# Sliding-window attention in rounded fp32: stacked query halves for the scores, split products for the values

## The chip, the cores and the metric

The kernel runs on one core of a Trainium2 chip. A core has a matrix engine (TensorE; "PE" in the profile, with its weight loads as "PEld"), two engines for element-wise work that read and write both memories (VectorE "DVE", ScalarE "ACT"), GpSimd ("POOL") and a queue that issues transfers (SyncE "SP"). They run side by side and meet at semaphores; each works through its own list of instructions in order. The metric is the device time of one execution in microseconds, as the median of several runs.

## The reference

A decoder trunk of two layers on one sequence of 256 tokens with 2048 features, all in fp32. Layer 0 is a recurrent block (RG-LRU) with a SwiGLU feed-forward part of 5632 features. Then one set of keys and values is projected. Layer 1 is grouped-query attention on a sliding window, with sinks, and again a feed-forward part. The change is in the keys and values and in the attention of layer 1:

```python
k = rms_norm(k.reshape(bsz, s, N_KV_HEADS, HEAD_DIM), k_g)      # 4 key heads of 64
v = v.reshape(bsz, s, N_KV_HEADS, HEAD_DIM)
...
q = rms_norm((h @ w_q).reshape(bsz, s, N_KV_HEADS, GROUP, HEAD_DIM), q_g)   # 32 query heads
scores = einsum("bnqhgd,bnkhd->bnhgqk", q, k_band) / sqrt(HEAD_DIM)
scores = where(window_mask(nblk), scores, -1e30)
probs = softmax(concatenate([scores, sink], axis=-1))[..., :-1]
out = einsum("bnhgqk,bnkhd->bnqhgd", probs, v_band)
return x + out.reshape(...) @ w_o
```

The band of a query block of 128 tokens is its own block and the one ahead of it. So the first block has 128 keys and the second 256.

## The kernel before

Activations lie with features in the 128 rows and the 256 tokens in the columns (T = 256). Weights come in tiles of 128 rows by 1024 columns, one tile per job; `stream` (L244) runs through the jobs, loads four tiles ahead and splits three ahead.

Each operand of a large product is split into a high part that rounded fp32 (fp32r) holds exactly and a low part with the rest. A product is then the sum of high times high, high times low and low times high. `split` (L236) does this for weights, with one ScalarE copy (L241) and one VectorE subtraction (L242) per tile; `split_act` (L321) does it for activations, high part in columns 0 to 255 and low part in columns 256 to 511 of a slot. The projections' products stand in `products` (L261, the products themselves on L269). A job of a projection is 24 products of 256 columns.

Everything else is a background task, written as a generator. `run_bg` (L192) is called twice in a job. It steps tasks as long as an estimated credit of VectorE and ScalarE time lasts; the helpers `a`, `tt`, `ts` and others add to the estimates, and `pe(ns)` takes off what TensorE spends on background products. From the key projection on, the credits are 740 and 900 ns per half job (`LATER`, L59). One way leads around the credit: `need(v)` (L205) is called by a job for its input and steps all tasks, whatever the credit, until that input is ready. Behind the generators the tile framework orders each engine's instructions and sets the waits.

The stage of the change has three parts. `kv` (L642), 8 jobs, projects keys and values. The keys of each key head are normalised, multiplied out of `sl` by a selecting matrix (L693) so that both 64-row halves of PSUM hold the same head, and split. Before, `kd[h]` is a pair of slots (high and low) in which rows 0 to 63 hold the keys in columns 0 to 255 and rows 64 to 127 hold them in columns 256 to 511, with zeros elsewhere; so one product gives the scores of two query heads. Values stay in fp32, 256 columns per token block.

`attn` (L758) has 32 jobs of w_q in four groups of eight, then w_o in four groups of eight. When a group of w_q ends, its `task` squares and splits the four tiles of q (two heads each), sums the squares on TensorE (L895, the group's statistics), makes the scales and spawns four `head_pair`s (L768), sixteen in all. A pair makes the scores of both token blocks (L784 to L786), scales them, adds the mask and takes the maximum (L798), takes the exponentials, scales by the reciprocal sums, transposes the probabilities (L832), copies them to a slot, multiplies by the values (L851 to L853, two heads into the two halves of the PSUM rows) and splits the result as `at[k]`. A job c of w_o's first group needs `at[2c]` and `at[2c+1]`; the last group of w_q ends just ahead of it.

PSUM has eight banks: four for the running group of a projection, up to four for the tasks.

## Time and profile before

| what | value |
|---|---|
| median of 3 runs | 1999.63 us (1999.16 to 2003.5) |
| profiled execution | 1999.26 us, span 1997.5 us |
| TensorE busy | 1987.8 us, 16795 instructions |
| VectorE busy | 1282.1 us |
| ScalarE busy | 1077.6 us |
| keys and values (first to last product) | 1018 to 1041.5 us |
| w_q and the head pairs | 1041.5 to 1206 us |
| granted TensorE clock | full throughout |

In the views below, a row of the timeline gives start, length, engine, line, operation, result and operands, shapes and count. Lengths of TensorE, VectorE and ScalarE instructions overlap those of their neighbours; what an instruction costs in a stream is the distance from its start to the next one's. In a line by form, the two numbers behind the bar are the busy time of the group and the mean length of one in ns. A plain fp32 product shows as two records, a rounded one as one.

### The profile page before, as it was taken

To read this page: it belongs to the slowest core of one execution; us is meant where nothing else is said; L and a number is where in the kernel's file an instruction comes from. 1 tells how busy PE (TensorE), PEld (TensorE's weight loads), DVE (VectorE), ACT (ScalarE), POOL (GpSimd) and SP (SyncE) were. 2 spreads that over 40 slices of the span, in tenths; PEclk is the share of its full clock that TensorE was granted. 3 is DMA by queue.
4 is the path that set the end of the run, shared out by engine and by line. 5 is a ranking of instruction groups with operands and counts; after the bars stand their busy time and mean duration, and the time that the engine had idled before them with its cause. 6 is when DMAs were issued, how large, how long until landed. Compare 5 with 4: busy or idle time off the path is not lost.

```text
span 1997.5 us, 40277 instructions
## 1 busy us (share of the span) xinstructions
PE 1987.8 (100%) x16795; PEld 1955.1 (98%) x16795; DVE 1282.1 (64%) x2062; ACT 1077.6 (54%) x1624; POOL 0.2 (0%) x4
## 2 busy tenths in 40 slices
PE   8999999999999999999999999999999999999999
PEld 8999999999999999999999999999999999999999
DVE  8989867556556656545768786765565566554543
ACT  7798655445444444434556775554454454444342
POOL 0000000000000000000000000000000000000000
PEclk9999999999999999999999999999999999999999
DMA  7655655655656566566564335655655665666663
GB/s 268 199 183 177 202 195 188 196 191 190 200 191 197 193 192 198 191 193 197 192 189 141 122 116 169 191 194 191 195 191 195 195 195 191 195 195 202 206 204 128
DMA packets 105015, 376.58 MB, mean 189 GB/s; under 512 B 11648, under 2 KB 13824, under 8 KB 104832
## 3 DMA queue, kind: packets, MB, share of 16 engines
q1 hardware_dynamic: 104832, 374.01, 58.1%
q8 instruction: 131, 2.15, 0.4%
q14 instruction: 52, 0.43, 0.1%
HBM read 371.86 MB, written 2.10 MB: 187 GB/s over the span
## 4 chain that ended last, share of the span: by engine, by line
PE 99%; ACT 0%; DMA 0%; DVE 0%; issue 0%
PE b L269 94%; PE b L545 1%; PE b L832 1%; PE b L740 1%; PE b L895 0%; PE b L851 0%; PE b L784 0%; PE b L786 0%; PE b L785 0%; PE b L853 0%; PE b L852 0%; PE b L749 0%; PE b L750 0%; PE b L751 0%; DMA x<-in_x 0%; ACT hi L241 0%
## 5 line engine op out<-in xcount | busy, mean ns | idle before, releaser
L269 PE MATMUL b<-s,hi 128*128 128x256 f32 (+1 forms) x10423 | 1430.2, 284 | 6.6 <-ACT hi L241 5.7
L269 PEld LDWEIGHTS b<-s,hi 128*128 128x128 f32 x10423 | 1322.5, 188 | 33.9 <-ACT hi L241 6.0
L242 DVE TENSOR_TENSOR lo<-raw,hi 128x1024 fp32r<-128x1024 f32 (+1 forms) x705 | 861.0, 1222 | 661.6 <-ACT hi L241 658.1
L241 ACT ACTIVATE hi<-raw 128x1024 fp32r<-128x1024 f32 (+1 forms) x705 | 746.1, 1059 | 774.7 <-PE b L269 744.3
L269 PE MATMUL b<-s,lo 128*128 128x256 f32 x5504 | 824.4, 277 | 0.0
L269 PEld LDWEIGHTS b<-s,lo 128*128 128x128 f32 x5504 | 716.4, 188 | 0.0
L105 ACT ACTIVATE t<-b 128x256 f32<-128x256 f32 x130 | 48.8, 384 | 62.2 <-PE b L269 37.9
L105 ACT ACTIVATE h<-h 128x256 f32<-128x256 f32 (+1 forms) x104 | 38.9, 375 | 21.1 <-DVE h L114 21.1
L105 ACT ACTIVATE s<-h 128x256 fp32r<-128x256 f32 (+1 forms) x106 | 42.7, 413 | 13.4 <-DVE h L114 10.9
L105 ACT ACTIVATE s<-s 128x256 f32<-128x256 f32 (+1 forms) x112 | 41.2, 415 | 4.0 <-DVE s L118 3.3
L114 DVE TENSOR_TENSOR h<-b,rstd 128x256 f32<-128x256 f32 x102 | 41.6, 415 | 0.0
L105 ACT ACT_TABLE_LOAD x31 | 39.8, 1283 | 1.3 <-PEq L1000 0.7
L114 DVE TENSOR_TENSOR h<-h,rstd 128x256 f32<-128x256 f32 x92 | 38.3, 420 | 1.5
L118 DVE SCALAR_TENSOR_TENSOR s<-x,par,s 128x256 fp32r<-128x256 f32 x80 | 36.7, 479 | 3.9 <-ACT s L105 3.9
L105 ACT ACTIVATE s<-x,par 128x256 fp32r<-128x256 f32 x80 | 37.9, 497 | 2.3 <-DVE x L114 1.8
L114 DVE TENSOR_TENSOR h<-b,t 128x256 f32<-128x256 f32 x90 | 37.5, 417 | 0.0
L114 DVE TENSOR_TENSOR s<-s,s 128x256 fp32r<-128x256 f32 (+1 forms) x80 | 31.0, 419 | 8.8 <-ACT s L105 8.6
L114 DVE TENSOR_TENSOR s<-h,s 128x256 fp32r<-128x256 f32 x88 | 36.6, 417 | 0.0
L114 DVE TENSOR_TENSOR h<-h,h 128x256 f32<-128x256 f32 x88 | 36.4, 415 | 0.1
L105 ACT ACTIVATE s<-b 128x384 f32<-128x384 f32 (+3 forms) x70 | 28.4, 428 | 10.3 <-PE b L853 5.6
L105 ACT ACTIVATE s<-s,h 128x128 f32<-128x128 f32 x64 | 28.3, 444 | 6.2 <-DVE h L123 6.2
L114 DVE TENSOR_TENSOR x<-x,b 128x256 f32<-128x256 f32 x64 | 25.2, 415 | 8.9 <-PE b L269 8.9
(99 smaller groups left out, 610.4 us busy)
## 6 DMA issues: line engine op xcount, KB each, us to landing
raw<-in_ffn_in SPq DMA_DIRECT2D x352, 512.0 KB, 3.5
raw<-in_ffn_out SPq DMA_DIRECT2D x176, 512.0 KB, 4.2
raw<-in_lru_in SPq DMA_DIRECT2D x63, 512.0 KB, 3.8
raw<-in_lru_out SPq DMA_DIRECT2D x32, 512.0 KB, 3.4
raw<-in_w_q SPq DMA_DIRECT2D x32, 512.0 KB, 3.3
raw<-in_w_o SPq DMA_DIRECT2D x32, 512.0 KB, 3.5
raw<-in_gate SPq DMA_DIRECT2D x8, 512.0 KB, 4.0
raw<-in_kv SPq DMA_DIRECT2D x8, 512.0 KB, 4.3
```

Source lines behind the costliest of these rows:

```text
L105: self.nc.scalar.activation(out, in_, func, **kw)
L114: self.nc.vector.tensor_tensor(out, a, b, op)
L118: self.nc.vector.scalar_tensor_tensor(out, a, s, b, op0, op1)
L241: self.nc.scalar.activation(hi[:, q], raw[:, q], AF.Copy)
L242: self.nc.vector.tensor_tensor(lo[:, q], raw[:, q], hi[:, q].bitcast(F32), ALU.subtract)
L269: self.nc.tensor.matmul(ps[f][:, 0:c1 - c0], w, x2[k][:, c0:c1], start=f not in begun, stop=last and all(q[1] != f for q in todo[n + 1:]))
L545: nc.tensor.matmul(ps[j][:, 0:T], (hi if high else lo)[:, c:c + P], x2[kt][:, q:q + T], start=kt == 0 and high > q, stop=kt == 1 and not high)
L740: nc.tensor.matmul(ps[f][:, 0:T], w0, x2[kt][:, q:q + T], start=k0 + kt == 0 and high > q, stop=k0 + kt == ND - 1 and not high)
L832: nc.tensor.transpose(p[:, j * P:(j + 1) * P], sc[hh][:, j * P:(j + 1) * P], one)
```

## The change

Keys. `kd[h]` becomes one slot: both 64-row halves hold the same keys, high parts in columns 0 to 255 and low parts in columns 256 to 511. The eight slots with zeros, and the clearing, are gone.

Queries. Each head of a tile of q gets its own 256 columns. Its high part lies in the 64 rows that it came in, its low part in the other 64. With such a block as weights, one product with the high keys gives high times high plus low times high in one sum over the rows, and one with the low keys adds the rest (low times low included). Per pair these are four products of 128 columns for the first token block and four of 256 for the second, in place of three of 256 and three of 512.

Values. They are scaled as before and then split, per key head 64 columns of high parts beside 64 of low parts. The transposed probabilities are split as well. The four transposes of each head's first two parts go to one bank, the two of the third to another. Their product with the values is: both value parts times the high probabilities (L852, 512 columns; L855, 256), and the high values times the low probabilities (L853, L854, weights of 64 columns). The result has its high-value part in PSUM rows 0 to 63 and its low-value part in rows 64 to 127. Two ScalarE copies and two VectorE adds of 64 rows join them for the two heads, and then the split follows.

```diff
             def task():
...
-                    self.ts(self.v[b].ap, self.v[b].ap, self.rstd[r][:, T + b:T + b + 1], None, ALU.mult)
+                    raw = vs[:, b * T:(b + 1) * T]
+                    self.ts(raw, raw, self.rstd[r][:, T + b:T + b + 1], None, ALU.mult)
+                    raw = raw.rearrange("p (h n) -> p h n", n=HD)
+                    q = self.v[b].ap.rearrange("p (h c n) -> p h c n", c=2, n=HD)
+                    self.a(q[:, :, 0], raw)
+                    self.tt(q[:, :, 1], raw, q[:, :, 0].bitcast(F32), ALU.subtract)
...
-                    kh, kl = self.kd[h].ap
-                    for i in range(2):
-                        q, c = slice(64 * i, 64 * i + 64), slice(i * T, i * T + T)
-                        self.a(kh[q, c], p[q, 0:T])
-                        self.tt(kl[q, c], p[q, 0:T], kh[q, c].bitcast(F32), ALU.subtract)
+                    self.split_act(self.kd[h].ap, p[:, 0:T])
...
-                o = p[:, 0:2 * n].rearrange("p (h n) -> p h n", h=2)
-                kh, kl = (q.rearrange("p (h n) -> p h n", h=2)[:, :, 0:n] for q in kd)
-                qh, ql = (qs[:, i * T + b * P:i * T + b * P + P] for i in range(2))
-                nc.tensor.matmul(o, qh, kh, start=True, stop=False)
-                nc.tensor.matmul(o, qh, kl, start=False, stop=False)
-                nc.tensor.matmul(o, ql, kh, start=False, stop=True)
+                for hh in range(2):
+                    q = qs[:, hh * T + b * P:hh * T + b * P + P]
+                    for i in range(2):
+                        nc.tensor.matmul(p[:, hh * n:(hh + 1) * n], q, kd[:, i * T:i * T + n], start=i == 0, stop=i == 1)
                 ps.append(p)
-                self.pe(330 * (b + 1))
+                self.pe(230 * (b + 1))
...
-            for hh in range(2):
-                s = self.slot(F32)
-                pT.append(s)
-                self.a(s[:, 0:384], ps[hh][:, 0:384])
-                self.free_mbank(ps[hh])
-                self.free(sc[hh])
-                yield
-            yield 1
+            while len(self.slots) < 3:
+                yield 1
+            ph, pl, p1 = (self.slot() for _ in range(3))
+            self.a(ph, ps[0])
+            self.tt(pl, ps[0], ph.bitcast(F32), ALU.subtract)
+            self.free_mbank(ps[0])
+            yield
+            self.split_act(p1, ps[1][:, 0:T])
+            self.free_mbank(ps[1])
...
-            for hh in range(2):
-                o, t = p[64 * hh:64 * hh + 64, :], pT[hh]
-                nc.tensor.matmul(o[:, 0:P], v0, t[:, 0:P], start=True, stop=True)
-                nc.tensor.matmul(o[:, P:T], v0, t[:, P:T], start=True, stop=False)
-                nc.tensor.matmul(o[:, P:T], v1, t[:, T:3 * P], start=False, stop=True)
-                self.free(t)
-                self.pe(400)
+            nc.tensor.matmul(p, v0, ph, start=True, stop=False)
+            nc.tensor.matmul(p[0:HD], v0[:, 0:HD], pl, start=False, stop=False)
+            nc.tensor.matmul(o[0:HD], v1[:, 0:HD], p1[:, T:2 * T], start=False, stop=False)
+            nc.tensor.matmul(o, v1, p1[:, 0:T], start=False, stop=True)
...
+            s, t = self.slot(), self.t()
             for hh in range(2):
+                self.a(t[HD * hh:HD * hh + HD], p[HD - HD * hh:P - HD * hh, hh * T:(hh + 1) * T])
+            for hh in range(2):
+                q = slice(HD * hh, HD * hh + HD)
+                self.tt(t[q], p[q, hh * T:(hh + 1) * T], t[q], ALU.add)
...
+            self.split_act(s, t)
...
-                        self.split_act(qs[f], v[f][:, 0:T])
+                        for hh in range(2):
+                            i, c = slice(HD * hh, HD * hh + HD), slice(hh * T, hh * T + T)
+                            self.a(qs[f][i, c], v[f][i, 0:T])
+                            self.tt(qs[f][HD - HD * hh:P - HD * hh, c], v[f][i, 0:T], qs[f][i, c].bitcast(F32),
+                                    ALU.subtract)
```

Two places show how this moves instructions. The first is TensorE's list in w_o's first group, at the statistics of the last four pairs. A name like `s_12058` is a slot with the number of its use, `hi` and `lo` are the weight buffers, which four jobs use in turn, `b` is a bank. Before:

```order
L269 MATMUL b_85<-s_12058,hi_76 128x256 x2
L269 MATMUL b_89<-s_12058,hi_76 128x256 x2
L269 MATMUL b_83<-s_12058,hi_76 128x256 x2
L269 MATMUL b_87<-s_12058,hi_76 128x256 x2
L269 MATMUL b_85<-s_12111,hi_76 128x256 x2
L269 MATMUL b_89<-s_12111,hi_76 128x256 x2
L895 MATMUL b_88<-con,s_12915 128x2 x2
L895 MATMUL b_88<-con,s_12918 128x2 x2
L895 MATMUL b_88<-con,s_12921 128x2 x2
L895 MATMUL b_88<-con,s_12923 128x2 x2
```

Here `s_12058` and `s_12111` are the third and fourth pair's results: the statistics stand within w_o's second job. After:

```order
L269 MATMUL b_83<-s_12693,lo_82 128x256
L269 MATMUL b_89<-s_12693,lo_82 128x256
L269 MATMUL b_90<-s_12693,lo_82 128x256
L852 MATMUL b_85<-s_13044,s_11065 128x512
L853 MATMUL b_85<-s_13045,s_11065 64x512
L854 MATMUL b_85<-s_13046,s_11066 64x2x128
L855 MATMUL b_85<-s_13046,s_11066 128x2x128
L907 MATMUL b_87<-con,s_12894 128x2 x2
L907 MATMUL b_87<-con,s_12897 128x2 x2
L907 MATMUL b_87<-con,s_12900 128x2 x2
L907 MATMUL b_87<-con,s_12902 128x2 x2
L269 MATMUL b_86<-s_12961,hi_75 128x256 x2
```

`s_12693` is the eighth pair's result and `s_12961` the ninth's: the statistics have moved behind the fourth job, ahead of the fifth.

The second place is VectorE's list where the last four pairs are worked on. Before, the splits of weights (L242) stand among the pairs' rows:

```order
L123 TENSOR_SCALAR s_13155<-s_13155,h_95 128x128
L123 TENSOR_SCALAR s_13155<-s_13155,h_95 128x256
L123 TENSOR_SCALAR s_13158<-s_13158,h_95 128x128
L123 TENSOR_SCALAR s_13158<-s_13158,h_95 128x256
L242 TENSOR_TENSOR lo_80<-raw_72,hi_76 128x1024
L114 TENSOR_TENSOR h_96<-h_96 128x4
L129 RECIPROCAL h_96<-h_96 128x4
L123 TENSOR_SCALAR s_13230<-s_13230,h_96 128x128
```

Between the last statistics and the last pair there are six such splits. After, three stand in all of it, and no other between the first two; the rows up to the second, with the last row of the twelfth pair (`s_13275`), are:

```order
L123 TENSOR_SCALAR s_13245<-s_13245,h_96 128x128
L114 TENSOR_TENSOR s_13319<-b_87,s_13318 128x512
L114 TENSOR_TENSOR s_13275<-t_91,s_13275 128x256
L123 TENSOR_SCALAR s_13245<-s_13245,h_96 128x256
L114 TENSOR_TENSOR s_13320<-b_88,s_13320 128x256
L114 TENSOR_TENSOR s_13338<-b_84,s_13337 128x512
L123 TENSOR_SCALAR s_13259<-s_13259,h_96 128x128
L123 TENSOR_SCALAR s_13259<-s_13259,h_96 128x256
L114 TENSOR_TENSOR s_13339<-b_85,s_13339 128x256
L242 TENSOR_TENSOR lo_80<-raw_72,hi_76 128x1024
```

What moved: the masks, scalings and splits of four pairs now stand together behind one split of weights, and the twelfth pair's result, which TensorE's sixth job of w_o needs, stands near their end. TensorE's list at that point:

```order
L828 MATMUL b_84<-con,s_13207 128x128 x2
L828 MATMUL b_85<-con,s_13199 128x128
L828 MATMUL b_85<-con,s_13207 128x128
L269 MATMUL b_83<-s_13275,hi_76 128x256
L269 MATMUL b_89<-s_13275,hi_76 128x256
L269 MATMUL b_90<-s_13275,hi_76 128x256
L852 MATMUL b_87<-s_13318,s_11065 128x512
L853 MATMUL b_87<-s_13319,s_11065 64x512
L269 MATMUL b_86<-s_13275,hi_76 128x512
```

The first product with `s_13275` stands behind the thirteenth and fourteenth pair's transposes and ahead of all later values.

More of the change, by code (lines that the diff above doesn't have):

```diff
@@ L825, in head_pair @@
             yield 1
-            ps, pT = [], []
-            for hh in range(2):
+            ps = []
+            for i in range(2):
                 while not self.room():
@@ L830, in head_pair @@
                 p = self.mbank()
-                for j in range(3):
-                    nc.tensor.transpose(p[:, j * P:(j + 1) * P], sc[hh][:, j * P:(j + 1) * P], one)
+                for hh in range(2):
+                    for j in ((0, 1), (2,))[i]:
+                        c = hh * T + j * P if j < 2 else hh * P
+                        nc.tensor.transpose(p[:, c:c + P], sc[hh][:, j * P:(j + 1) * P], one)
                 ps.append(p)
-                self.pe(400)
+                self.pe(530 - 265 * i)
             yield 1
-            for hh in range(2):
-                s = self.slot(F32)
-                pT.append(s)
-                self.a(s[:, 0:384], ps[hh][:, 0:384])
-                self.free_mbank(ps[hh])
-                self.free(sc[hh])
-                yield
-            yield 1
+            while len(self.slots) < 3:
[7 more added lines that the diff above has]
+            self.free_mbank(ps[1])
+            for s in sc:
+                self.free(s)
+            yield 2
             while not self.room():
@@ L885, in task @@
                         qs.append(self.slot())
[L886 removed]
+                        for hh in range(2):
+                            i, c = slice(HD * hh, HD * hh + HD), slice(hh * T, hh * T + T)
+                            self.a(qs[f][i, c], v[f][i, 0:T])
+                            self.tt(qs[f][HD - HD * hh:P - HD * hh, c], v[f][i, 0:T], qs[f][i, c].bitcast(F32),
+                                    ALU.subtract)
                         yield
```

30 lines of the change are left out of this document (13 added, 17 removed).

## The prediction

> **What bounds the kernel now.** I read the page's engine totals first, then the chain of work that ended last, then what TensorE waited for.
>
> ```profile
> span 1997.5 us, 40277 instructions
> PE 1987.8 (100%) x16795; PEld 1955.1 (98%) x16795; DVE 1282.1 (64%) x2062; ACT 1077.6 (54%) x1624; POOL 0.2 (0%) x4
> ...
> PE 99%; ACT 0%; DMA 0%; DVE 0%; issue 0%
> ...
> PE b L269 <- ACT hi L241: 5.7, 1, 5.7
> PE b L269 <- ACT s L105: 0.9, 1, 0.9
> ```
>
> TensorE is on the chain for 99% of the span and waits 6.6 us in all, once at the start. So a TensorE microsecond saved is a microsecond saved, as long as nobody makes TensorE wait. The change touches attention alone, so the next view is the busy time there: four stretches over the sixteen head pairs, and one of the feed-forward layer ahead of them.
>
> ```profile
> 900.00:1018.00 118.00, 118.00 (x1028) 117.38 (x1027) 69.71 (x93) 56.60 (x75) 0.00 (x0) 1.00 0.60 193
> ...
> 1076.00:1111.00 35.00, 35.00 (x290) 32.98 (x290) 27.37 (x92) 26.62 (x72) 0.00 (x0) 1.00 0.35 112
> 1111.00:1146.00 35.00, 35.00 (x295) 33.10 (x294) 26.96 (x91) 26.71 (x71) 0.00 (x0) 1.00 0.37 121
> 1146.00:1182.00 36.00, 36.00 (x300) 33.90 (x299) 27.65 (x92) 27.76 (x73) 0.00 (x0) 1.00 0.37 118
> 1182.00:1206.00 24.00, 24.00 (x206) 22.33 (x205) 20.56 (x79) 18.65 (x55) 0.00 (x0) 1.00 0.34 111
> ```
>
> After the TensorE columns come VectorE and ScalarE. In the feed-forward layer VectorE is busy 59%. Over these 130 us it is busy 27.37 + 26.96 + 27.65 + 20.56 = 102.5 us, 79%, and ScalarE 99.7 us. VectorE's reserve is 27.5 us. That number decides the case.
>
> **TensorE, part by part.** Starts of consecutive products give the price of each, since their recorded durations overlap.
>
> ```profile
> 1001.91 1.98 PE L269 MATMUL b<-s,hi 128*128 128x256 f32 x16
> 1003.72 1.07 PE L269 MATMUL b<-s,lo 128*128 128x256 f32 x8
> ...
> 1063.12 0.59 PE L693 MATMUL b<-s,con 128*128 128x256 f32 x2
> ...
> 1063.79 0.28 PE L269 MATMUL b<-s,lo 128*128 128x256 f32 x1
> ...
> 1076.52 0.28 PE L784 MATMUL b<-s,s 128*128 128x256 f32 x1
> ...
> 1076.87 0.40 PE L784 MATMUL b<-s,s 128*128 128x512 f32 x1
> ...
> 1077.57 2.04 PE L269 MATMUL b<-s,hi 128*128 128x256 f32 x16
> ...
> 1106.00 1.87 PEld L895 LDWEIGHTS b<-con,s 128*128 128x128 f32 x16
> 1107.79 0.30 PEld L269 LDWEIGHTS b<-s,hi 128*128 128x128 f32 x2
> ```
>
> A 256-column product costs 1.81 / 16 = 0.113 us. The scores of a pair take 1.05 us: three products of 256 columns at 0.117 and three of 512 at 0.233. Afterwards the second block needs four of 256 columns, 4 x 0.117 = 0.47. The first needs four of 128 columns in rounded fp32, a form that the trace lacks. Its low end is half a 256-column product, 0.06. Its high end is plain fp32: the L693 product and two L269 products fill 1063.12 to 1063.79, so the former takes 0.67 - 0.23 = 0.44 for 256 columns and 0.22 for 128. I take 0.11. L895 moves only two columns, yet its weight loads follow each other every 1.79 / 16 = 0.112 us, and each of the new products reloads 128 columns of weights too. So 0.45 + 0.47 = 0.92, a gain of 0.13 per pair, 2.1 us for sixteen. At the ends of the price a pair gains 0.33 or loses 0.30.
>
> A rule of the Trainium skill would be kinder. "TensorE: Matmul & The Clock Gate", section "Back-to-back issue gap", gives about 81 ns per product of 128 columns in a stream with weight loads; by that the four cost 0.32, and sixteen pairs gain 2 us more. Its section "LDWEIGHTS" has 128 columns load at 128 / 1.2 = 107 ns, which this trace's 112 ns bears out for fp32, and therefore I stay with the row.
>
> Probabilities times values comes next. Eight pairs do it alone, eight two at a time:
>
> ```profile
> 1134.67 0.28 PE L269 MATMUL b<-s,lo 128*128 128x256 f32 x1
> 1134.88 0.43 PE L851 MATMUL b<-s,s 128*64 128x128 f32 x2
> ...
> 1135.64 0.38 PE L853 MATMUL b<-s,s 128*64 128x128 f32 x2
> 1135.95 0.51 PE L269 MATMUL b<-s,hi 128*128 128x256 f32 x2
> ...
> 1122.43 0.40 PE L786 MATMUL b<-s,s 128*128 128x512 f32 x1
> ...
> 1124.49 0.50 PE L269 MATMUL b<-s,hi 128*128 128x512 f32 x1
> ```
>
> Alone it takes 1.28 - 0.11 = 1.17 us; doubled, (2.06 - 0.23) / 2 = 0.92 each; together 8 x 1.17 + 8 x 0.92 = 16.7 us. The new form has two products of 512 and two of 256 columns, 0.70 us. The middle two use 64 columns of the array. Entering that form costs 0.21 instead of 0.11 before the first L851, and leaving it as much, so two changes add 0.19: 0.89 per pair, 14.2 us, a gain of 2.5. With free changes it is 3 us more; with dearer ones, twice that, 3 us less.
>
> The tiling page of the Trainium skill ("TensorEngine Tiling (Array Packing)", "Key Properties") says that a change of tiling mode drains the engine. The 0.10 us is what such a drain costs here. By that rule every pair now pays it twice, where doubled pairs paid once each, which is in the sum.
>
> Transposes stay six a pair. TensorE's own work falls by 2.1 + 2.5 = 4.6 us.
>
> **VectorE.** Its prices, again from start to start:
>
> ```profile
> 1113.03 0.54 DVE L798 CUSTOM_DVE_ANT_0 s<-b,con,par 128x256 f32<-128x256 f32 x1
> ...
> 1113.50 0.41 DVE L798 CUSTOM_DVE_ANT_0 s<-b,con,par 128x128 f32<-128x128 f32 x1
> 1113.83 0.08 DVE L798 DVE_READ_ACCUMULATOR2_ANT h<- 128x1 f32 x1
> ...
> 1114.30 1.22 DVE L242 TENSOR_TENSOR lo<-raw,hi 128x1024 fp32r<-128x1024 f32 x1
> 1115.44 0.17 DVE L123 TENSOR_SCALAR h<-h 128x4 f32<-128x4 f32 x1
> ...
> 1119.56 0.16 DVE L114 TENSOR_TENSOR h<-h 128x4 f32<-128x4 f32 x1 [0.50 <-ACT s L105]
> 1119.75 0.18 DVE L129 RECIPROCAL h<-h 128x4 f32<-128x4 f32 x1
> ...
> 1196.33 0.75 DVE L114 TENSOR_TENSOR s<-b,s 128x256 fp32r<-128x256 f32 x2
> 1196.99 0.40 DVE L798 CUSTOM_DVE_ANT_0 s<-b,con,par 128x128 f32<-128x128 f32 x1
> ...
> 1199.19 1.00 DVE L123 TENSOR_SCALAR s<-s,h 128x128 f32<-128x128 f32 x4
> 1200.11 1.22 DVE L242 TENSOR_TENSOR lo<-raw,hi 128x1024 fp32r<-128x1024 f32 x1
> ...
> L114 DVE TENSOR_TENSOR s<-b,s 128x256 fp32r<-128x256 f32 x15 | 5.9, 418 | 4.3 <-ACT s L105 4.3
> ...
> L114 DVE TENSOR_TENSOR s<-b,s 64x256 fp32r<-64x256 f32 x8 | 3.4, 421 | 0.4 <-ACT s L105 0.2
> ...
> L105 ACT ACTIVATE s<-b 128x256 fp32r<-128x256 f32 x16 | 6.1, 384 | 5.7 <-PE b L853 5.6
> ```
>
> So a tensor-tensor operation of 256 elements takes 0.33 us, of 1024 1.14, and by a third of the difference, 0.60 for 512. A masked maximum takes 0.33 or 0.47, four scalings of probabilities 0.92. A pair adds the low part of the probabilities (0.60 and 0.33), the two adds that join the halves (2 x 0.33) and one more operation in q's split (0.33; 64 rows take 421 ns where 128 take 418): 1.93 us, 31 us for sixteen pairs, against a reserve of 27.5. The cleared key halves save some memsets ahead of this stage, where nothing waits for them. ScalarE gains two copies per pair for the halves and one for q's split, 3 x 0.38 = 1.1 us, while its copies of the probabilities hold 768 elements as before: 18 us on 99.7, which still fits into 130.
>
> VectorE does not wait with this work to the end of the stage. The credit that paces background work spreads the pairs, and they slip: the statistics of the last four pairs (L895, now L907) stood in the second job of w_o's first group and now stand after the fourth. The deadline did not slip. The sixth job needs the twelfth pair, and the forced stepping then puts all that is left of the pairs between two splits of weights. From the statistics to the last row for the twelfth pair (s_13275 in the changed order) VectorE has one split (1.14), sixteen maxima (8 x 0.33 + 8 x 0.47 = 6.4), seventeen scalings (3.9), two operations of 512 (1.2), five of 256 (1.7) and 27 small ones, which take about 0.17 (0.19 between the starts of the two on h) and together 4.6: 18.9 us. In the same place TensorE has the fifth job (2.7), a third of the sixth (0.9), scores of four pairs (3.7), eighteen transposes at 0.105 (1.9) and one set of values (0.9): 10.1 us. It then stands at the product with s_13275. That is a wait of 8.8 us. Behind it in TensorE's queue is everything else, weights of later jobs included. After it, VectorE needs 10.1 us to the last pair, TensorE has 13.3, so only the chain of that last pair may show: 0 to 2, I take 1. The same count in the kernel before gives VectorE 20.9 us from the statistics to the sixteenth pair and TensorE 27, hence no wait, as the trace has it. In the rest of the stage VectorE runs at some 90%; I take 1 us, with 0 to 5 as bounds.
>
> Sum: -4.6 + 8.8 + 1 + 1 = +6.2 us on the profiled execution's 1999.26 (span 1997.5 and 1.8 around it). The median of the runs lies 0.4 higher: 2006.
>
> **Rivals.**
> Faster: the wait stays under 4.6 us. That happens if VectorE gets through the last four pairs in 14 us instead of 18.9, or starts them 4 us earlier against TensorE. Then 1995 with no wait at all. For it: 27 small operations priced by few rows. Against it: the operation counts, and a queue that works in order.
> No measurable change: half the wait, since w_o's later products were pulled ahead of it. Then 2000. For it: the changed order does so in a few places, such as the second group's first products ahead of the first group's last. Against it: at the product with s_13275 nothing free stands in front.
> Four passes for the 128-column products: 0.22 each. Only the twelve pairs ahead of the last four pay, since TensorE waits there anyway: 12 x (0.13 + 0.30) = 5.2 us, 2011. Against it: the 256-column form shows one pass.
> VectorE late throughout: of its 27.5 us idle, part was waiting inside the softmax chains, which stays. If a third, 9 us, can't be filled, the 102.5 + 31 us need 142 us, not 130. That is 12 us more, and with 1 us for the last pair's chain 2013.
>
> **How the numbers follow.** My forecast has 0.50, the late VectorE 0.17, four passes 0.13, no change 0.14, faster 0.06. A change within 0.2% (4 us) is about what a measurement of this kernel can't tell from none. A little of the forecast's own spread (2003 to 2009) falls inside that bound, so slower has 0.76, the same 0.18, faster 0.06. The range runs from the no-change case, 1999, to just past the late VectorE, 2014.
>
> **What would show it.** Right: a TensorE wait of about 9 us on VectorE's rows in w_o's first group, near the sixth job; score products of 128 columns 0.11 apart; 0.9 us per set of values; VectorE near 90% over the stage. Wrong: no wait over 3 us there; 128-column starts 0.06 or 0.22 apart; waits spread over all sixteen pairs, or on ScalarE.

## The result, and the profile after

The changed kernel takes 2016.11 us (median of 3 runs, 2014.81 to 2017.91) against 1999.63: a ratio of 1.008, with an interval of 1.0067 to 1.0094. That is 16.5 us slower. I had forecast 2006, slower, with a range from 1999 to 2014, so the measured time lies beyond its end.

The profiled execution took 2017.91 us, 18.6 more than that of the kernel before. Of these, 3.5 us arise before the 40th job, in code that the change doesn't touch; four of the eighteen profiled executions here have such a late start (the change, e1, e2 and e14), and the kernel before has runs up to 2003.5. So 15.1 us are to be explained, and the lowest runs of both kernels, 15.65 apart, say the same.

First the totals and the chain of work that ended last, of the changed kernel:

```profile
span 2016.1 us, 40221 instructions
PE 1995.4 (99%) x16699; PEld 1958.3 (97%) x16699; DVE 1311.4 (65%) x2124; ACT 1095.2 (54%) x1670; POOL 0.2 (0%) x4
...
PE 93%; ACT 3%; DVE 3%; issue 1%; DMA 0%; SPq 0%; ACTq 0%; DVEq 0%
```

TensorE held 99% of the chain before; now 6% of it runs over ScalarE and VectorE. TensorE is idle for 2016.1 - 1995.4 = 20.7 us, where it was for 9.7. The stretches of the stage (length, then busy time of PE, PEld, DVE, ACT, POOL, then granted clock, DMA share and rate) show where:

```profile
1076.00:1111.00 35.00, 34.01 (x268) 31.88 (x268) 31.67 (x103) 26.15 (x72) 0.00 (x0) 1.00 0.37 121
1111.00:1146.00 35.00, 33.58 (x266) 31.49 (x265) 32.82 (x106) 29.36 (x78) 0.00 (x0) 1.00 0.37 118
1146.00:1182.00 36.00, 34.38 (x265) 31.91 (x263) 32.73 (x95) 31.43 (x80) 0.00 (x0) 1.00 0.38 121
1182.00:1200.00 18.00, 15.37 (x118) 14.00 (x119) 16.44 (x47) 12.27 (x26) 0.00 (x0) 1.00 0.46 147
1200.00:1206.00 6.00, 5.37 (x24) 4.68 (x22) 6.00 (x37) 3.66 (x19) 0.00 (x0) 0.59 0.01 3
1206.00:1212.00 6.00, 3.56 (x15) 2.11 (x14) 5.78 (x29) 5.87 (x26) 0.00 (x0) 0.78 0.00 0
1212.00:1218.00 6.00, 5.39 (x29) 4.55 (x29) 4.80 (x11) 3.73 (x9) 0.00 (x0) 0.77 0.01 3
```

Three things are to be seen. TensorE, busy for the whole of each stretch before, now lacks 1.0, 1.4 and 1.6 us in the first three: it waits from the first pairs on, not at one place. (Its count of instructions, 268 for 290 in the first row, says less, since a pair now has 18 records for 24.) VectorE is busy 90 to 94% up to 1200 us. And in the last three rows TensorE executes 68 products in 18 us at a granted clock of 0.59 to 0.78, while VectorE is full until 1212 and hardly any weights move. That is the foreseen wait at w_o's sixth job:

```profile
1188.83 1.84 PE L907 MATMUL b<-con,s 128*128 128x2 f32 x16
1190.53 2.13 PE L269 MATMUL b<-s,hi 128*128 128x256 f32 x16
...
1195.96 1.08 PE L269 MATMUL b<-s,hi 128*128 128x256 f32 x4 [1.45 <-ACT s L105]
...
1199.23 1.18 PE L780 MATMUL b<-s,s 128*128 128x128 f32 x8 [1.19 <-DVE s L114]
1201.04 3.82 PE L780 MATMUL b<-s,s 128*128 128x128 f32 x16 [0.63 <-DVE h L792]
...
1211.23 0.61 PE L828 MATMUL b<-con,s 128*128 128x128 f32 x2 [1.86 <-DVE t L114]
1211.81 1.01 PE L269 MATMUL b<-s,hi 128*128 128x256 f32 x3
...
1213.61 1.25 PE L269 MATMUL b<-s,hi 128*128 128x512 f32 x4
```

The last statistics end at 1188.83 + 1.84 = 1190.67. The three products at 1211.81 are the first with the twelfth pair: in the order of the instructions they stand just behind these transposes, and they read its high part alone. The first product that also reads its low part opens the row at 1213.61, behind a set of values. VectorE in the same place, and the ScalarE copy that makes that high part:

```profile
1193.11 0.36 DVE L125 TENSOR_SCALAR rr<-b,r 128x8 f32<-128x8 f32 x2
...
1211.36 0.40 ACT L105 ACTIVATE s<-t 128x256 fp32r<-128x256 f32 x1
...
1212.45 0.41 DVE L114 TENSOR_TENSOR s<-t,s 128x256 fp32r<-128x256 f32 x1
```

VectorE needs 19.7 us from the statistics to the end of the last row for the twelfth pair, the subtraction for its low part. The waits between 1070 and 1230 us (engine, operand, line, what it waited for and its line: total, times, longest) are many and short:

```profile
PEld b L828 <- DVE s L123: 4.2, 7, 1.3
PEld b L828 <- ACT s L105: 3.0, 2, 2.0
PEld b L269 <- ACT s L105: 3.0, 5, 1.7
PEld b L780 <- DVE s L114: 1.8, 2, 1.4
```

Transposes (L828) wait for the scaled probabilities, w_o's products (L269) for a pair's result, scores (L780) for q's low part. The products themselves cost what their forms say:

```profile
1080.07 1.08 PE L780 MATMUL b<-s,s 128*128 128x128 f32 x8
1080.99 2.05 PE L269 MATMUL b<-s,hi 128*128 128x256 f32 x16
...
1113.22 0.39 PE L852 MATMUL b<-s,s 128*128 128x512 f32 x1
1113.45 0.40 PE L853 MATMUL b<-s,s 128*64 128x512 f32 x1
1113.69 0.28 PE L854 MATMUL b<-s,s 128*64 128x256 f32 x1
1113.80 0.28 PE L855 MATMUL b<-s,s 128*128 128x256 f32 x1
1113.92 1.58 PE L269 MATMUL b<-s,hi 128*128 128x256 f32 x12
```

Scores take 1080.99 - 1080.07 = 0.92 us a pair, as forecast; values 1113.92 - 1113.22 = 0.70, not 0.89. So TensorE's own work fell by 16 x 0.13 + 16.7 - 16 x 0.70 = 7.6 us (7.8 with the unrounded rows; the expectations below use that), and the waits cost some 23.

### The profile page after: what moved, and what is told of

Its sections match the earlier page's. It is cut to its first block, busy times and chain, and to the rows that moved or that the text cites. A ratio compares the mean times of both kernels' runs of the same rounds, so it can differ in the third digit from the quotient of the medians.

```text
span 2016.1 us, 40221 instructions
## 1 busy us (share of the span) xinstructions
PE 1995.4 (99%) x16699; PEld 1958.3 (97%) x16699; DVE 1311.4 (65%) x2124; ACT 1095.2 (54%) x1670; POOL 0.2 (0%) x4
## 4 chain that ended last, share of the span: by engine, by line
PE 93%; ACT 3%; DVE 3%; issue 1%; DMA 0%; SPq 0%; ACTq 0%; DVEq 0%
PE b L269 90%; ACT s L105 2%; ACT hi L241 1%; DVE s L792 1%; DVE lo L242 1%; PE b L735 1%; PE b L545 0%; PE b L828 0%; PE b L907 0%; DMA raw<-in_lru_in 0%; DVE s L114 0%; ACT L105 0%; PE b L780 0%; DVE s L118 0%; DVE s L123 0%
## 5 line engine op out<-in xcount | busy, mean ns | idle before, releaser
L269 PE MATMUL b<-s,hi 128*128 128x256 f32 (+1 forms) x10423 | 1436.8, 284 | 9.7 <-ACT hi L241 5.9
L269 PEld LDWEIGHTS b<-s,hi 128*128 128x128 f32 x10423 | 1325.3, 188 | 38.1 <-ACT hi L241 6.7
L242 DVE TENSOR_TENSOR lo<-raw,hi 128x1024 fp32r<-128x1024 f32 (+1 forms) x705 | 861.5, 1222 | 663.4 <-ACT hi L241 660.1
L269 PE MATMUL b<-s,lo 128*128 128x256 f32 x5504 | 823.1, 277 | 0.0
L269 PEld LDWEIGHTS b<-s,lo 128*128 128x128 f32 x5504 | 716.5, 188 | 0.0
L105 ACT ACTIVATE t<-b 128x256 f32<-128x256 f32 (+1 forms) x162 | 61.2, 384 | 67.0 <-PE b L269 36.8
L105 ACT ACTIVATE s<-s 128x256 f32<-128x256 f32 (+2 forms) x130 | 48.3, 414 | 2.7 <-DVE s L118 1.9
L114 DVE TENSOR_TENSOR s<-s,s 128x256 fp32r<-128x256 f32 (+2 forms) x98 | 38.7, 419 | 6.6 <-ACT s L105 5.7
L792 DVE CUSTOM_DVE_ANT_0 s<-b,con,par 128x128 f32<-128x128 f32 x64 | 26.9, 474 | 0.1
```

The lines of the kernel that those rows point to most:

```text
L105: self.nc.scalar.activation(out, in_, func, **kw)
L114: self.nc.vector.tensor_tensor(out, a, b, op)
L242: self.nc.vector.tensor_tensor(lo[:, q], raw[:, q], hi[:, q].bitcast(F32), ALU.subtract)
L269: self.nc.tensor.matmul(ps[f][:, 0:c1 - c0], w, x2[k][:, c0:c1], start=f not in begun, stop=last and all(q[1] != f for q in todo[n + 1:]))
L792: nc.vector.tensor_tensor_reduce(s[:, c0:c1], ps[b][:, hh * (c1 - c0):(hh + 1) * (c1 - c0)], con[:, K_MASK + c0:K_MASK + c1], rr[:, b * 8 ...
```

## Experiments

Each row below has a run's median, the ratio to the kernel before with its interval (each compared with runs of the kernel before on the same chip, whose medians lie between 1999.57 and 2000.5), and ahead of them how far the busy time of the two engines over the whole profiled execution stands above that of the kernel before (1282.1 and 1077.6 us), from the totals of the pages. A busy time counts an operation's whole length, so it can differ by a few microseconds from a sum of prices taken from start to start.

| run | what it is | VectorE busy, us | ScalarE busy, us | median, us | ratio |
|---|---|---|---|---|---|
| after | the change | +29 | +18 | 2016.11 | 1.008 (1.0067 to 1.0094) |
| e1 | scores alone | +2 | +5 | 2003.63 | 1.0019 (1.001 to 1.0029) |
| e2 | values alone | +25 | +12 | 2012.17 | 1.0059 (1.0044 to 1.0074) |
| e3 | larger credit | +29 | +19 | 2018.98 | 1.0094 (1.0079 to 1.0109) |
| e4 | no low part of the probabilities, still charged | +15 | +18 | 2009.18 | 1.0043 (1.0026 to 1.006) |
| e5 | the old account | +28 | +17 | 2011.67 | 1.006 (1.0043 to 1.0077) |
| e6 | e4, not charged | +15 | +18 | 2007.41 | 1.0039 (1.0024 to 1.0054) |
| e7 | scalings on GpSimd | +18 | +19 | 2053.57 | 1.0268 (1.0252 to 1.0283) |
| e8 | e1 with the old account | +2 | +6 | 1998.99 | 0.9998 (0.9989 to 1.0007) |
| e9 | e5 without the low part | +14 | +17 | 2007.63 | 1.0039 (1.0024 to 1.0054) |
| e10 | e9 without the joining adds | +2 | +17 | 2002.83 | 1.0016 (1.0006 to 1.0025) |
| e11 | e10 without the joining copies | +2 | +5 | 1995.3 | 0.9977 (0.9968 to 0.9987) |
| e12 | e5, three subtractions per pair on GpSimd | +17 | +18 | 2012.51 | 1.0062 (1.0047 to 1.0077) |
| e13 | e11 and two copies aside, most of them ahead of the stage | +2 | +18 | 1999.16 | 0.9989 (0.998 to 0.9999) |
| e14 | e11 and five additions aside, many ahead of the stage | +24 | +5 | 2000.89 | 0.9996 (0.9987 to 1.0006) |
| e15 | e11 and two copies aside | +1 | +18 | 2003.98 | 1.0015 (1.0005 to 1.0026) |
| e16 | e11 and five additions aside | +26 | +5 | 2006.37 | 1.0032 (1.0017 to 1.0046) |

Where the time is lost along the way is read from the starts of the same job in two traces: how many us later it starts than in the kernel before (w_q is jobs 376 to 407, w_o's first group 408 to 415):

```
job    after     e5     e9    e11    e16     e8
376     3.59   0.28   0.48   0.23   0.70   0.51
392     2.64   0.84   0.35  -0.01   0.46   1.83
400     1.13   2.94  -0.76  -2.09   0.23   0.32
408    -0.15   5.37  -0.46  -2.94   0.08   0.28
412     2.70   5.86   0.64  -3.17   1.90   0.18
418    18.62  12.39   7.62  -3.62   7.09   0.27
440    18.62  12.08   7.91  -3.62   7.09  -0.04
```

### The halves, the credit and the low part

Theory A: the added VectorE work costs the time. Theory B: the account of pacing does, because it makes the last pairs slip towards w_o's deadline. Theory C, here: the new score products are slow. e1 is the change's keys, queries and scores with the old values, e2 the reverse:

```diff
 e1
-                self.pe(330 * (b + 1))
+                self.pe(230 * (b + 1))
...
+                        for hh in range(2):
+                            i, c = slice(HD * hh, HD * hh + HD), slice(hh * T, hh * T + T)
+                            self.a(qs[f][i, c], v[f][i, 0:T])
...
 e2
+            nc.tensor.matmul(p, v0, ph, start=True, stop=False)
+            nc.tensor.matmul(p[0:HD], v0[:, 0:HD], pl, start=False, stop=False)
...
 e3 (on the change)
-    LATER = (740.0, 900.0, 1000.0)
+    LATER = (1100.0, 1300.0, 1400.0)
 e4 (on the change)
-            self.tt(pl, ps[0], ph.bitcast(F32), ALU.subtract)
+            self.dve += 69 + 1.042 * 2 * T
...
-            self.split_act(p1, ps[1][:, 0:T])
+            self.a(p1[:, 0:T], ps[1][:, 0:T])
+            self.dve += 69 + 1.042 * T
```

In e4 the products with the low part read the high part instead, so the low part's contribution is missing.

> Only the score half of the change: doubled keys, query halves stacked, scores of 4 products of 128 and 4 of 256 columns; values and probabilities as in the kernel before. TensorE's list gets shorter by 0.13 us per pair, 2.1 us in all; VectorE gets one more operation of 0.33 us per pair, 5 us in all, against 27 us that it had idle. Theory A (VectorE's added work of 1.9 us per pair is what costs the time) and theory B (the pacing credit, which lets the last pairs slip, costs it) both expect 0.5 to 2.5 us faster than before, 1997 to 1999. Theory C (the score form itself is slow, for instance by its 128-column products) expects 4 us slower or more.

> Only the value half: V_hi beside V_lo as weights, split probabilities, joining copies and adds; scores as in the kernel before. TensorE saves about 5.7 us (0.69 for a set of values against 1.17 alone and 0.92 doubled), VectorE gains 1.6 us per pair, 26 us. Theories A and B expect most of the loss here: 8 to 16 us slower than before, with the waits in w_o's first group and TensorE's clock granted at half after them. Theory C expects it faster than before by 3 to 6 us.

> The whole change, with the credits per half job raised from 740 and 900 to 1100 and 1300 ns (and the credit that may be saved up from 1000 to 1400), so that the background work is let in sooner; no operation is added or removed. Theory B expects the wait in w_o's first group to fall from 15 us to under 4 and the time to come to 2001 or less. Theory A expects the same VectorE work to make TensorE wait elsewhere: the wait in w_o's first group halves, waits in w_q grow, and the time stays at 2008 or more.

> The whole change without the two subtractions that make the low part of the probabilities (0.60 and 0.33 us per pair, 15 us of VectorE in all); the products that would read the low part read the high part instead, so TensorE's list is the same. The credit is still charged for them, so the pairs stand in the same jobs. The result lacks the low part. Theory A expects the time to fall by most of what the change cost: 2003 or less. Theory B expects the last pairs to stay late in w_o's first group and the wait there to fall only by the operations left out ahead of it: 2010 or more.

The values carry most of it: e2 costs 12 us of the 16.5. e1 was a miss for A and B: 4 us slower, about as C had it, though its VectorE work hardly grew; the score products themselves took 0.92 us a pair in the change, so e1's loss needs another source, and e8 below finds it. e3 let the pairs in sooner and halved the longest stretch of VectorE work between two splits (20.4 to 10.5 us in the order), yet it was 3 us slower than the change: its jobs fall back by 6.7 us within w_q (from 376 to 408), where the change gains 3.7. e4 got back 7 us for 15 of VectorE work, less than A had expected.

### The account by itself

e5 is the change with every operation, but charged as the kernel before charges a pair. e8 does that to e1, e6 takes the kept charge out of e4. Theory S in the expectations is B by another name.

```diff
 e5 (on the change; the added subtractions, copies and adds are issued without being charged)
-                self.pe(230 * (b + 1))
+                self.pe(330 * (b + 1))
...
-                self.pe(530 - 265 * i)
+                self.pe(400)
...
-            self.pe(680)
+            self.pe(800)
 e6 (on e4)
-            self.dve += 69 + 1.042 * 2 * T
...
-            self.dve += 69 + 1.042 * T
 e8 (on e1)
-                self.pe(230 * (b + 1))
+                self.pe(330 * (b + 1))
...
+                            if hh:
+                                self.dve -= 69 + 1.042 * T
+                                self.act -= 100 + 0.833 * T
```

> The changed kernel with every one of its operations, but accounted for as the kernel before accounts for a pair: 2590 ns of TensorE credit instead of 2165, and nothing charged for the subtractions, copies and adds that were added. Statistics of the last four pairs go back to between w_o's first and second job (they stood after the fourth), and the longest stretch of VectorE work between two splits falls from 20.4 to 8.3 us in the order. Theory S (the slip of the last pairs to a fixed deadline costs the time): 1999 to 2004. Theory A (the amount of VectorE work costs it, wherever it stands): 2011 to 2018.

> The changed kernel without the two subtractions that make the low part of the probabilities (15 us of VectorE work; the products on the low part read the high part instead), and this time without their charge. Leaves out the low part's contribution. Statistics of the last four pairs stand one job earlier than in the changed kernel, longest stretch of VectorE work between two splits 7.7 us. Beside the run that kept the charge (2009.2) it tells the slip from the work: theory S expects 1997 to 2002, theory A about what the kept charge gave, 2007 to 2011. If it stays over 2004, neither carries it and the longer chain of a pair is next.

> The half with the scores alone (it gave 2003.6), with the old account: 330 ns of TensorE credit per block of a product instead of 230 and nothing charged for the second copy and subtraction in q's split. Same operations. If the 4 us of that half came from where its pairs were put (S): 1997 to 2000. If they come from its operations (A, or the form of the scores itself): 2002 to 2005.

The account costs 4.6 us in the half with the scores (2003.63 to 1998.99, all of its loss), 4.4 in the whole change, 1.8 without the low part. By their bounds e5 and e6 came out where A had them, e8 where S had it. So the account counts, but it isn't the case. The table of starts shows why: in e5 the last group falls back by 6.5 us between jobs 412 and 418 instead of 15.9, while it loses 5.6 from job 376 to 412, where the change had gained 0.9. Waits of e5 between 1070 and 1230 us, with L837 the subtraction for the low part and L853 the first product with the values:

```profile
PEld b L853 <- DVE s L837: 4.7, 4, 2.8
PEld b L269 <- ACT s L105: 3.9, 3, 2.8
PEld b L853 <- ACT s L105: 3.2, 4, 1.5
PEld b L854 <- DVE s L837: 1.8, 2, 1.4
```

Work that is not put off to the end is waited for earlier.

### Taking the added work away, step by step

From e5, e9 leaves out the two subtractions for the low part of the probabilities, e10 also the two adds that join the halves, e11 also the two copies ahead of them. TensorE's products keep their number and shapes, and the account is that of e5. Theory V is A again (VectorE's amount); theory C now stands for ScalarE's copies and a pair's longer end.

```diff
 e9
-            nc.vector.tensor_tensor(pl, ps[0], ph.bitcast(F32), ALU.subtract)
...
-            nc.vector.tensor_tensor(p1[:, T:2 * T], ps[1][:, 0:T], p1[:, 0:T].bitcast(F32), ALU.subtract)
 e10
-                nc.vector.tensor_tensor(t[q], p[q, hh * T:(hh + 1) * T], t[q], ALU.add)
 e11
-                nc.scalar.activation(t[HD * hh:HD * hh + HD], p[HD - HD * hh:P - HD * hh, hh * T:(hh + 1) * T], AF.Copy)
...
-            self.split_act(s, t)
+            self.split_act(s, p[:, 0:T])
```

> A series with the order of the old account (which gave 2011.7), taking away one added kind of work after the other at the same TensorE list, 7.8 us shorter than before. First step: without the two subtractions for the low part of the probabilities (leaves out their contribution), VectorE 15 us less, still 13 us over before; ScalarE as in the changed kernel, 13 us over before. Theory V (VectorE's amount): two fifths to a half of what it loses by going from the full kernel to the bare one, so 2002 to 2005. Theory C (ScalarE's copies and the longer end of a pair: copies, adds, copy, subtraction): 2006 to 2011.

> Second step: the two adds that join the halves are left out too (the result then holds only one half of the values product). VectorE 2 us over before, ScalarE still 13 us over. Theory V: 1992 to 1997, the whole gain of TensorE's list is there. Theory C: still 2001 to 2008.

> Third step: the two copies of the halves are left out as well (the result then holds the values product of the high part alone, for the first head of a pair). VectorE 2 us and ScalarE 4 us over before, a pair ends as before. Both theories: 1991 to 1996. If it stays over 1998, the shorter TensorE list itself doesn't turn into time, for a reason outside VectorE and ScalarE.

The steps give 4.0 us for 15 of VectorE work, 4.8 for 10.7 of it, and 7.5 for about 12 of ScalarE work (busy 1095.0 us in e10, 1082.9 in e11). V missed e9 and e10, so VectorE isn't all. C's bounds held, but if the copies were all, e9 and e10 would have stayed near e5, and they lie 4.0 and 8.8 us below it. (The runs of e10 spread from 1999.2 to 2006.8 and its profile is of the lowest, so no row of its stage is read here. That lowest run alone has a mean granted clock of 1.000; the nine others have 0.998 or 0.999. So part of the 7.5 comes with a fall of the clock; which of the two brings the other isn't shown.) With both gone, 4.8 of the 7.6 us that TensorE saves appear, and only these waits of any size are left in e11:

```profile
PEld b L828 <- DVE s L123: 2.1, 6, 0.6
PEld b L851 <- ACT s L105: 1.1, 4, 0.4
```

### Amount or place

The operations taken away were also steps of a pair's chain. To tell the two apart, e11 got work of the same size that nobody reads. In e13 and e14 it reads a constant; in e15 and e16 it reads the pair's result:

```diff
 e13 (on e11)
+                nc.scalar.activation(t[HD * hh:HD * hh + HD], con[HD * hh:HD * hh + HD, 0:T], AF.Copy)
 e14 (on e11)
+            for n in (T, T, T, T, T):
+                nc.vector.tensor_tensor(t, con[:, 0:T], con[:, 0:T], ALU.add)
 e15 (on e11)
+                nc.scalar.activation(t[HD * hh:HD * hh + HD], s[HD * hh:HD * hh + HD, T:2 * T].bitcast(F32), AF.Copy)
 e16 (on e11)
+            for n in (T, T, T, T, T):
+                nc.vector.tensor_tensor(t, s[:, T:2 * T].bitcast(F32), s[:, 0:T].bitcast(F32), ALU.add)
```

> The last step of the series (1995.3) with two copies of 64x256 on ScalarE put back per pair, but aside: they come behind the pair's last operation, read a constant, and nobody reads what they write. The result is as in that step. The account of pacing doesn't know them. If the two copies of the halves cost their 7.5 us by their amount of ScalarE work (9.9 us in all): 2000 to 2004. If they cost it as steps of each pair's last stretch, from values to w_o, whatever their amount: 1995 to 1998.

> The last step of the series (1995.3) with five additions of 256 elements per pair on VectorE aside, behind the pair's last operation, read by nobody: 26.7 us, about what the subtractions of the low part and the two joining adds took away (25.6). If VectorE's amount of work as such is what these cost (8.8 us in the series): 2002 to 2006. If it is their place in a pair's chain: 1995 to 1999.

> As the two copies aside (1999.2), but the copies read the pair's own result, so that they can't be placed ahead of it: the trace of that run shows most of its copies before the pairs began, from 1026 us on, where they test little. Nobody reads what they write; 9.9 us of ScalarE inside the stage. If the two joining copies cost their 7.5 us by ScalarE's amount: 2000 to 2004. If as steps of the pair's last stretch: 1995 to 1998.

> As the five additions aside (2000.9), but reading the pair's own result, so that all 26.7 us of VectorE stand inside the stage. If VectorE's amount is what the subtractions and joining adds cost (8.8 us in the series): 2003 to 2008. If their place in the chain: 1995 to 2000.

e13 and e14 don't tell it: they came out between both theories, and their copies and additions start at 1026.5 and 1023.3 us, 50 us ahead of the first pair. What depends on nothing, the framework puts where the engines are still free. In e15 the copies run from 1089.9 to 1209.3 us, 0.41 us each:

```profile
L866 ACT ACTIVATE t<-s x32: 399/414/419, 1089.9 to 1209.3; 64x256 f32<-64x256 f32 x32
```

e15 loses 8.7 us on e11, where the joining copies had cost 7.5; e16 loses 11.1 us for 26.7 of VectorE work, where the subtractions and adds had cost 8.8 for 25.6. Nobody waits for the added operations; they only stand in the queues of the two engines. So amount alone is enough to cost this much, on either engine, and a place in a pair's chain isn't needed for it.

Three things limit the figures. The runs of e15 fall into two kinds: five with a mean granted clock of 1.000 take 2000.9 to 2003.4 us, and five with 0.998 or 0.999 take 2004.5 to 2008.4. The profile is of the first kind, 2001.15, 5.5 us above that of e11, so the 8.7 of the medians comes with falls of the clock in half of the runs. Then, three of e15's copies stand at the head of ScalarE's queue until VectorE has made what they read, 1.6 us in all. And the lists of e11, e15 and e16 differ in more than the added operations, since the framework orders them anew: counted in L269's products, TensorE has the last group's first transposes 36.5 jobs into w_q and w_o in e11, 37.7 in e15 and 38.0 in e16. What each of these is worth wasn't separated.

The same 130 us (1076 to 1206, with the columns as above), one row for each kernel.

e11:

```profile
1076.00:1206.00 130.00, 129.10 (x1016) 121.17 (x1016) 110.19 (x371) 106.42 (x285) 0.00 (x0) 1.00 0.38 125
```

e15:

```profile
1076.00:1206.00 130.00, 125.58 (x982) 116.84 (x980) 105.03 (x361) 113.46 (x303) 0.00 (x0) 1.00 0.38 121
```

e16:

```profile
1076.00:1206.00 130.00, 124.14 (x964) 114.91 (x962) 122.28 (x417) 98.45 (x264) 0.00 (x0) 1.00 0.37 117
```

In 130 us e15 gets 34 products fewer done than e11, with ScalarE at 113.46 / 130 = 87%; e16 gets 52 fewer, with VectorE at 94%. Neither engine is full.

### The idle engine

GpSimd does nothing in this kernel. e7 gives it the 64 scalings of the probabilities (on the change), e12 the subtractions that read no PSUM (on e5):

```diff
 e7
-                    self.ts(o, o, den[:, i:i + 1], None, ALU.mult)
+                    nc.gpsimd.tensor_scalar(o, o, den[:, i:i + 1], None, ALU.mult)
 e12
-                            self.tt(qs[f][HD - HD * hh:P - HD * hh, c], v[f][i, 0:T], qs[f][i, c].bitcast(F32),
-                                    ALU.subtract)
+                            nc.gpsimd.tensor_tensor(qs[f][HD - HD * hh:P - HD * hh, c], v[f][i, 0:T],
+                                                    qs[f][i, c].bitcast(F32), ALU.subtract)
...
-            self.split_act(s, t)
+            self.a(s[:, 0:T], t)
+            nc.gpsimd.tensor_tensor(s[:, T:2 * T], t, s[:, 0:T].bitcast(F32), ALU.subtract)
```

> The changed kernel, complete, but the four scalings of the probabilities of each pair (64 in all, 14.7 us of VectorE work) run on GpSimd, which does nothing else in this kernel; they are not charged to VectorE's account. If A and S together are right and GpSimd takes up to 1 us for one scaling, about what the last experiment gives, 1997 to 2004. If GpSimd is slow (over 2 us for one) or holds VectorE up, the chain of a pair gets longer: 2008 to 2020.

> The complete changed kernel with the old account, with those of its subtractions that read no accumulator on GpSimd: q's low part (two per pair) and the low part of a pair's result. VectorE 11 to 12 us over before, ScalarE 13 us over. At about 0.8 us per operation on GpSimd, off the chain of a pair for q: theory V 2002 to 2006, theory C 2006 to 2012; 2012 to 2018 if GpSimd's operations come late for the statistics and for w_o.

e7 lies far beyond both of its bounds. Two groups of it by form (busy time and mean ns behind the bar), and what the transposes waited for:

```profile
L816 POOL TENSOR_SCALAR s<-s,h 128x256 f32<-128x256 f32 x32 | 31.4, 981 | 0.0
L816 POOL TENSOR_SCALAR s<-s,h 128x128 f32<-128x128 f32 x32 | 22.7, 708 | 1205.9 <-DVE h L129 1129.6 <-ACT s L105 76.3
```

```profile
PEld b L828 <- POOL s L816: 36.8, 49, 2.1
```

A scaling takes 0.84 us on the average where four take 0.92 on VectorE, and all four stand between the maxima and the transposes. e12 took its work from places that are less pressed, and still gained nothing on e5. Groups of VectorE between 1076 and 1206 us in e5 and then in e12:

```profile
L242 DVE TENSOR_TENSOR lo<-raw,hi 128x1024 fp32r<-128x1024 f32 x27 | 32.9, 1222 | 0.4 <-ACT hi L241 0.2
...
L123 DVE TENSOR_SCALAR h<-h 128x4 f32<-128x4 f32 x15 | 2.4, 163 | 0.1
```

```profile
L242 DVE TENSOR_TENSOR lo<-raw,hi 128x1024 fp32r<-128x1024 f32 x27 | 34.3, 1272 | 3.5 <-ACT hi L241 3.4
...
L123 DVE TENSOR_SCALAR h<-h 128x4 f32<-128x4 f32 x14 | 3.2, 231 | 0.1
```

Some of VectorE's operations get longer beside a working GpSimd: its busy time falls by 11.5 us from e5 to e12 (1310.4 to 1298.9), where 48 subtractions at 0.33 are 16. Why the other 11.5 gained nothing isn't shown; e9, with 14 us off VectorE, had gained 4.0, and TensorE's weight loads wait only 1.0 us for GpSimd in e12. No complete kernel of these beats the one before; e8 equals it.

## Why the prediction was wrong

**What held.** TensorE as the bound before; the score products at 0.11 and 0.92 us a pair; VectorE at some 90% over the stage; the slip of the last pairs to the sixth job, with 19.7 us of VectorE work there against 18.9 forecast and 9.9 of TensorE's against 10.1 (a set of values took 0.70 and not 0.9).

**The values were sized too dear.** "Two changes add 0.19" was wrong: 0.70 us, not 0.89, 3 us in all to the good. The page "TensorEngine Tiling (Array Packing)" of the Trainium skill, section "Key Properties", says that a change of tiling mode drains the engine. The rows at 1113.22 to 1113.92 show no such time for 64 columns of weights between two products with 128. The 0.10 us of the kernel before stood beside plain fp32 products into both halves of the PSUM rows; which of the two differences matters wasn't tested.

**The wait at the sixth job was sized too small.** 11.2 us (1190.7 to 1211.8, less 9.9 of work), not 8.8. VectorE reached the statistics only at 1193.1, 2.4 us after they were ready, since it was behind already, and its work there was 0.8 longer. Nor did the wait end where I had it end, at VectorE's last row for the twelfth pair: the first three products with that pair read only its high part, which ScalarE copies at 1211.36, ahead of that row. Behind it TensorE's starts exceed the prices of its products by about 4.1 us more up to 1230, for which I took 1; part of that is the clock, which stood at a half from 1211.4 to 1214.6.

**The step that failed** is "In the rest of the stage VectorE runs at some 90%; I take 1 us, with 0 to 5 as bounds", and with it the sentence that ScalarE's 18 us "still fits into 130" and so costs nothing. Between jobs 376 and 412 the waits took about 8.5 us, counted as what the distances between TensorE's starts exceed the prices of its products. -7.6 + 11.2 + 4.1 + 8.5 makes 16.2; measured are 15.1, and I leave the difference to the prices.

Both terms, VectorE's and ScalarE's, come to one thing. A reserve of 27.5 us in 130 is not work that can be added free of charge: an operation put into the queue of VectorE or ScalarE delays whatever stands behind it, TensorE's list is in a fixed order, and so every transpose and score whose operands come late stops it. e15 and e16 show the price with operations that nobody waits for: by the medians 8.7 us for 12 of busy time on ScalarE and 11.1 for 24 on VectorE, on engines that were 82% and 85% busy in e11. Together that is 19.8 us on e11's 1995.3. e5 holds about the work of both (26 us of busy time on VectorE and 12 on ScalarE beyond e11's) and lies 16.4 above it. By the profiled runs the prices are 5.5 and 10.7 us, 0.45 us per microsecond of busy time on either engine; that ScalarE's time is dearer isn't shown.

The rival "VectorE late throughout" (2013, given 0.17) was the nearest in time, and the nearest in reason: from 1076 to 1206 us VectorE still has 10.3 us idle (it is busy 119.66), about the 9 that it took for unfillable. That this idle time lies inside the softmax chains wasn't measured, and ScalarE isn't in that rival. With ScalarE in it, it should have been the forecast. As I took the slip for the cause, I had waits at one place. e5 and e3 show that the place only sets where the waits appear: pairs let in sooner are waited for in w_q. What the slip and the changed account are worth by themselves is 4.4 us.

## What to carry to other kernels

When a kernel's bound engine has a fixed list, price work added to its helpers at a good part of its length even where they show a fifth of idle time, on each of them, and add a single late wait on top only if the pairs that run into it aren't the same work counted again. Before trading helper work for TensorE time, put the helper work in alone, aside and reading the real data, and see what it costs: here 12 us on ScalarE alone cost 5.5 to 8.7, about the 7.6 us of products saved. Look at the granted clock of every run, too: every run of e15 with a lowered clock took longer than every run without. The changed pacing account moved the pairs later on all engines here, and cost 4.4 us of its own.

## What the runs showed of the hardware

The granted clock fell to 0.59, 0.78 and 0.77 in the three stretches from 1200 to 1218 us, where TensorE had waited much: 0.41 + 0.22 + 0.23 of 6 us each, 5.2 us of full-speed work, inside the 15.3 counted for the tail (11.2 + 4.1). In narrower stretches the profile gives 0.50 for 1201.2 to 1207.8, 1.00 for 1208 to 1211.2 and 0.50 for 1211.4 to 1214.6: it is a halved clock, for some 10.3 us. The Trainium skill has half the clock after an idle window of about 3.4 us and back after as long a busy one ("TensorE: Matmul & The Clock Gate", section "What's actually happening"). The trace agrees with the halving, but no single idle time of TensorE is that long there: the longest is 1.45 us ahead of the first fall and 1.86 ahead of the second, and from 1190 to 1201 TensorE was idle for 3.2 us of 11 in pieces with work between them.

GpSimd needs 0.71 us for a scaling of 128 elements and 0.98 for 256. While it worked, VectorE's operations on 4 columns took 231 ns instead of 163.
